# Later weight loads of the projections issued from ScalarE's queue instead of SyncE's

## The chip, the cores and the metric

The kernel runs on one core of a Trainium2 chip. What is measured is the device time of one execution in microseconds (us); before the change its median is 1826.89 us over three runs, which lie between 1826.79 and 1827.04. The engines are called as in the profile: PE (TensorE, matmuls) and PEld (its weight loads), DVE (VectorE), ACT (ScalarE), POOL (GpSimd) and SP (SyncE, which computes nothing and here issues DMA transfers). ACT can issue transfers too, from its own queue. Each engine works through its instructions in their order and waits where one of them needs another engine or a transfer.

## The reference

One layer of a decoder: a combined input projection feeds three token mixers, whose outputs go through one output projection, and a SwiGLU feed-forward network follows. There are 512 tokens of width 2048, all in float32.

```python
h = _rms_norm(x, norm1_g[l])
proj = h @ w_in[l]                                   # 2048 -> 3840 columns
aq, ak, av, bu, bg, cq, ck, cv = jnp.split(proj, splits, axis=-1)
out_a = _dilated_mixture(aq, ak, av)                 # 8 heads, three window/dilation patterns
out_b = _conformer_conv(bu, bg, ...)                 # GLU, 31-tap causal conv, LayerNorm, swish
out_c, _ = _band_attention(cq, ck, cv, ..., sinks)   # 16 query heads on 2 kv heads, window 128
x = x + concatenate([out_a, out_b, out_c]) @ w_out[l]
h2 = _rms_norm(x, norm2_g[l])
x = x + (silu(h2 @ w_gate[l]) * (h2 @ w_up[l])) @ w_down[l]
```

The queries and keys of a and c are normalised per head.

## The kernel before, in words

Activations lie with channels on the 128 partitions and the 512 tokens along them. Every float32 product is made of three matmuls: an operand is split into a high part (a cast to the matmul's own format) and a low part (what the cast left over), and `mm3` (lines 328 to 330) multiplies high by high, high by low and low by high.

**Stages.** Until about 50 us the first four column tiles of the input projection run together, k by k, as x arrives. Then `project` makes the other 26 column tiles one after the other (to about 375 us). Into these matmuls the attention of heads c and a, the convolution's taps and the normalisations are woven: a list of due times (`Ticks`) calls their pieces, one tick for every two k steps of a projection. Most pieces that move data across partitions go through DRAM and back (tiles named ..d and ..t, such as `c4ed` and `a1et`), by transfers that SP issues. The output projection follows (tiles named `o`, about 375 to 563 us) in two halves of sixteen tiles, each half over eight of the sixteen mixer rows; `residual` (line 1166) adds a finished bank into `xr`, the rows of x. The feed-forward network takes the rest, in seven products per block with sums and differences of weights made by POOL.

**Weights.** A weight unit is a tile of 128 x 1024 float32, 512 KB in one transfer (the first five are parts of such a tile). Units 0 to 10 are the first four column tiles, units 11 to 62 the other 26, two each, and units 63 to 94 the output projection, one per tile and half. Units of the feed-forward network have tuples as keys. Each unit has a raw buffer assigned beforehand (`RAW_PLAIN`, `RAW_FEWER`; from unit 51 to 90 five buffers in turn, since the attention of heads a uses two of the others). A unit's way is this: `pump` (line 237) takes its buffer if that is free and issues the load on line 249; `split_up_to` (line 269) has ACT cast the high part, `wh` (line 295), and keeps the subtraction of the low part in a list; `lows_now` (line 259) has DVE subtract, `wl` (named by line 269 in the profile); and PE multiplies. The split runs two units ahead of use (`SPLIT_AHEAD`), into three buffers each for `wh` and `wl`, so that a cast also waits until PE has finished a unit three back.

**Order around a load.** During the projections (`cooling`) `lows_now` is called in the middle of a unit; it frees buffers that were split one or two units before, pumps, and then subtracts. In the output projection nothing cools. `next_unit` runs in this order there:

```python
lows_now()                    # DVE subtracts the unit split last; its buffer is free; pump loads into it
split_up_to(u + SPLIT_AHEAD)  # ACT casts the next unit
```

Every load names an engine whose queue issues it, `eng` of `pump`. It is SP in all but the first call, where ACT issues four loads. A load waits in its queue until its buffer's last reader, the subtraction, is done. Transfers signal their end on eight semaphores that are handed out in turn, and a transfer also waits for the one before it on its semaphore.

The names that come up below: `c4e`, the exponentials of a pair of c heads on ACT (line 884); `c7by`, their scales spread over partitions by a transfer (line 842); `c4pl`, low parts of weights that POOL masks (line 935) for PE's `c4o` (line 1031); `a1et`, weights of an a pair coming back from DRAM (line 983), and `a1ph`, ACT's cast of them (line 993); `mh_c` and `ml_c`, the split mixer rows (lines 1085 and 1086).

Of the kernel before, what the change touches and what calls it, by code (L numbers as in the profile page):

```python
# [60 lines left out]
SPLIT_BUFS = 3  # L61
X_AHEAD = 8
SPLIT_AHEAD = 2
WARM = 8


# [55 lines left out]
def kernel(ctx: ExitStack, tc: tile.TileContext, xT, wi, wo, wgu, wd, cst_in, outT):  # L122
    nc = tc.nc
# [22 lines left out]
    def bank(name, cols=T, pool="banks"):  # L146
        return psum[pool].tile([P, cols], F32, name=name, tag="b")
# [11 lines left out]
    def take(buf, key, n=1024):  # L159
        assert buf not in held  # L160
        held[buf] = key
        raws[key] = (wp.tile([P, 1024], F32, name=f"w{key}", tag=f"raw{buf}", bufs=1), n)
        return raws[key][0]
# [25 lines left out]
    for n in range(2 * NBLOCKS):  # L189
# [6 lines left out]
        for i, c in enumerate("AB"):  # L196
            key = keys[c]
# [43 lines left out]
    def pump(limit, most=99, eng=nc.sync):  # L241
        while at["entry"] < len(entries) and len(raws) < limit and entries[at["entry"]][0] not in held and most:
            most -= 1
            buf, key, parts = entries[at["entry"]]
            size = [part.shape[-1] * (part.shape[1] if len(part.shape) == 3 else 1) for part in parts]
            t, o = take(buf, key, sum(size)), 0
            for part, n in zip(parts, size):
                to = t[:, o:o + n]
                eng.dma_start(to.rearrange("p (n f) -> p n f", n=part.shape[1]) if len(part.shape) == 3 else to, part)
                o += n  # L250
            at["entry"] += 1

# [10 lines left out]
    def lows_now():  # L263
        if lows and cooling:
            release()
            pump(RAW_EARLY if at["use"] <= 20 else RAW_BUFS)
        while lows:
            fn, *args = lows.pop(0)
            fn(*args)  # L269
        if late_lows and not cooling:  # L270
            pump(RAW_EARLY if at["use"] <= 20 else RAW_BUFS)

    def split_up_to(i):
        while at["split"] <= min(i, len(works) - 1):
            key, last, eng = works[at["split"]]
            of = [b for b, k in held.items() if k == key]
            t, n = drop(key) if last else raws[key]
            if cooling:
                held.update((b, None) for b in of)
                cool.extend(of)  # L280
            u = at["split"]
            hi = wp.tile([P, 1024], F32R, name=f"wh{u}", tag="hi", bufs=SPLIT_BUFS)
            lo = wp.tile([P, 1024], F32R, name=f"wl{u}", tag="lo", bufs=SPLIT_BUFS)
            if eng == "moves":

                near = psum["high"].tile([P, 1024], F32R, name=f"wn{u}", tag="h")
                src = t[:, :n].rearrange("p (n f c) -> p f n c", n=4, c=P)
                by = lambda x: x[:, :n].rearrange("p (f n c) -> p f n c", n=4, c=P)
                nc.scalar.copy(by(near), src)
                nc.scalar.copy(by(hi), src)  # L290
                nc.vector.tensor_sub(by(lo), src, by(near).bitcast(F32))
            elif eng or "high" not in psum:
                eng = eng or nc.vector

                (nc.vector.tensor_copy if u == 0 else nc.scalar.copy)(hi[:, :n], t[:, :n])  # L295
                lows.append((eng.tensor_sub, lo[:, :n], t[:, :n], hi[:, :n].bitcast(F32)))
                if not late_lows:
                    lows_now()
            else:
                near = psum["high"].tile([P, 1024], F32R, name=f"wn{u}", tag="h")  # L300
                nc.scalar.copy(near[:, :n], t[:, :n])
                nc.scalar.copy(hi[:, :n], t[:, :n])
                lows.append((nc.vector.tensor_sub, lo[:, :n], t[:, :n], near[:, :n].bitcast(F32)))
                if not late_lows:
                    lows_now()
            splits[u] = (hi, lo)
            at["split"] += 1
# [5 lines left out]
    def next_unit():  # L313
        sums_now()
        u = at["use"]
        at["use"] += 1
        moves = works[u][2] == "moves"
        ahead = moves and u < turned_to
        if ahead:
            pump(RAW_BUFS, 2)  # L320
        lows_now()
        split_up_to(u + SPLIT_AHEAD)
        if not lows and not ahead:
            pump(RAW_EARLY if u < 20 else RAW_BUFS, 2 if moves else 99)
        return splits.pop(u)
# [26 lines left out]
    b = bank("idle")  # L352
    for i in range(WARM):
        nc.tensor.matmul(b, idle, idle[:, None, :].to_broadcast([P, NT, P]), start=True, stop=True)
# [890 lines left out]

    split_up_to(at["use"] + SPLIT_AHEAD - 1)
    ticks.tick()
    split_up_to(at["use"] + SPLIT_AHEAD)
    b = m_hi = m_lo = r1b = bias_a = bias_c = over = upper = None
# [30 lines left out]
    def run(queue):  # L1280

        for fn, *args in queue.pop(0) if queue else ():
            fn(*args)
# [231 lines left out]
    for n in range(NBLOCKS):  # L1515
        blk = Up(n)
        for blk.first in (0, 4):
            for i, q in enumerate(ORDER):
                for c, _ in enumerate(blk.product(q)):
# [5 lines left out]
                    if 1 <= n <= 8 and at_unit in (9, 23):  # L1525
                        key = SUMS[2 * n - 2 + at_unit // 16]
# [32 lines left out]
    class Down:  # L1559
# [9 lines left out]
        def product(self, k, q):  # L1569
# [5 lines left out]
            for c in range(2):  # L1575
                sums_now()
                if self.end and k == 5:
                    split_up_to(at["use"] + SPLIT_AHEAD)
                run(evacs)
# [62 lines left out]
        def sum(self, i, k, a):  # L1642
            return self.g, i, k, a
# [149 lines left out]
```

## Time and profile before

| | |
|---|---|
| median of the runs | 1826.89 us |
| profiled execution: its own time | 1827.03 us |
| its span, first to last instruction | 1825.3 us |
| mean granted clock of TensorE | 0.999 |
| DMA queue q1 (SP): packets, MB | 408576, 352.12 |
| DMA queue q10 (ACT): packets, MB | 576, 0.79 |
| moved bytes over the span | 194 GB/s |

The profile is one execution. A row of a timeline gives start and duration in us, engine, line, operation and the tiles written and read; a remark in brackets gives the idle time before and what ended it. A row of waits has who waited, for whom, the sum in us, how often, and the longest. SPq and ACTq are the queues' own instructions: the issue of a transfer (DMA_DIRECT2D) and waiting for a semaphore (EVENT_SEMAPHORE), which are not counted as busy time.

### The profile page before, as it was taken

The numbers are of one execution on the slowest core, as the hardware profiler recorded it, in microseconds if no ns is written. First come the engines' busy times: TensorE is split into PE (matmuls) and PEld (weight loads), VectorE is DVE, ScalarE is ACT, GpSimd is POOL, SyncE is SP. The second block draws the span as 40 slices with busy tenths as digits, with TensorE's granted clock in tenths as the row PEclk, the third lists the DMA queues.
The fourth block names the chain that finished last, engine by engine and source line by source line (L and its number), as shares of the span: only waits on it lengthen the run. The fifth ranks groups of instructions, "written<-read, shape, count | busy, mean of one in ns | idle before, by whom it ended". The sixth has DMA issues, their size and how long they took to land.

```text
span 1825.3 us, 26570 instructions
## 1 busy us (share of the span) xinstructions
PE 1818.3 (100%) x8191; PEld 1509.9 (83%) x8191; DVE 1434.5 (79%) x1996; ACT 1327.6 (73%) x1848; POOL 1022.1 (56%) x793
## 2 busy tenths in 40 slices
PE   9999999999999999999999999999999999999998
PEld 7888888888888888888888888888888888888887
DVE  6779999987689777777777777777777777777777
ACT  6345656664468778888888888888887778877775
POOL 0116555120014577786887868878775568775652
PEclk9999999999999999999999999999999999999999
DMA  7355456666343557787777877778687579877645
GB/s 279 96 161 157 152 172 182 195 211 214 130 145 113 130 142 206 191 222 192 194 205 191 220 192 197 204 190 223 176 278 261 195 230 293 259 256 255 231 127 105
DMA packets 409295, 354.61 MB, mean 194 GB/s; under 512 B 177088, under 2 KB 331840, under 8 KB 409152
## 3 DMA queue, kind: packets, MB, share of 16 engines
q1 hardware_dynamic: 408576, 352.12, 65.7%
q8 instruction: 65, 1.06, 0.2%
q10 hardware_dynamic: 576, 0.79, 0.1%
q14 instruction: 78, 0.64, 0.1%
HBM read 270.00 MB, written 74.41 MB: 189 GB/s over the span
## 4 chain that ended last, share of the span: by engine, by line
PE 99%; DVE 1%; DMA 0%; issue 0%; ACT 0%; SPq 0%; DVEq 0%; ACTq 0%
PE out L1374 15%; PE out L1375 15%; PE out L1372 15%; PE out L1637 7%; PE out L1639 7%; PE out L1638 7%; PE o L328 3%; PE o L330 3%; PE o L329 3%; PE cq L328 2%; PE cq L329 2%; PE cq L330 2%; PE ak L328 1%; PE aq L328 1%; PE av L328 1%; PE ak L330 1%
## 5 line engine op out<-in xcount | busy, mean ns | idle before, releaser
L1372 PE MATMUL out<-wh,h 128*128 128x512 f32 x1232 | 479.2, 389 | 0.0
L1374 PE MATMUL out<-wl,h 128*128 128x512 f32 x1232 | 479.2, 389 | 0.0
L1375 PE MATMUL out<-wh,h 128*128 128x512 f32 x1232 | 479.2, 389 | 0.0
L1372 PEld LDWEIGHTS out<-wh,h 128*128 128x128 f32 x1232 | 231.2, 188 | 48.1
L1374 PEld LDWEIGHTS out<-wl,h 128*128 128x128 f32 x1232 | 231.2, 188 | 48.1
L1375 PEld LDWEIGHTS out<-wh,h 128*128 128x128 f32 x1232 | 231.2, 188 | 47.9
L1637 PE MATMUL out<-wh,a 128*128 128x512 f32 x620 | 240.4, 388 | 0.0
L1638 PE MATMUL out<-wl,a 128*128 128x512 f32 x620 | 240.3, 388 | 0.0
L1639 PE MATMUL out<-wh,a 128*128 128x512 f32 x620 | 240.3, 388 | 0.0
L295 ACT CAST wh<-w 128x1024 fp32r<-128x1024 f32 (+2 forms) x94 | 97.0, 1032 | 115.8 <-PE o L329 48.9
L1647 DVE TENSOR_TENSOR y<-y,out 128x512 f32<-128x512 f32 x192 | 128.6, 684 | 47.6 <-PE out L1639 46.1
L269 DVE TENSOR_TENSOR wl<-w,wh 128x1024 fp32r<-128x1024 f32 (+2 forms) x95 | 114.1, 1203 | 30.0 <-ACT wh L295 28.9
L1639 PEld LDWEIGHTS out<-wh,a 128*128 128x128 f32 x620 | 116.4, 188 | 24.0
L1638 PEld LDWEIGHTS out<-wl,a 128*128 128x128 f32 x620 | 116.4, 188 | 23.8
L1637 PEld LDWEIGHTS out<-wh,a 128*128 128x128 f32 x620 | 116.4, 188 | 23.8
L590 DVE SCALAR_TENSOR_TENSOR y<-bu,cst,y 128x511 f32<-128x511 f32 (+14 forms) x120 | 89.8, 748 | 0.5
L328 PE MATMUL o<-mh_c,wh 128*128 128x512 f32 x128 | 50.3, 393 | 0.0
L328 PE MATMUL cq<-hh,wh 128*128 128x512 f32 x128 | 50.0, 391 | 0.0
L329 PE MATMUL cq<-hl,wh 128*128 128x512 f32 x128 | 49.9, 390 | 0.0
L329 PE MATMUL o<-ml_c,wh 128*128 128x512 f32 x128 | 49.9, 390 | 0.0
L330 PE MATMUL o<-mh_c,wl 128*128 128x512 f32 x128 | 49.9, 390 | 0.0
L330 PE MATMUL cq<-hh,wl 128*128 128x512 f32 x128 | 49.8, 389 | 0.0
(2359 smaller groups left out, 4736.4 us busy)
## 6 DMA issues: line engine op xcount, KB each, us to landing
od<-a SPq DMA_DIRECT2D x154, 256.0 KB
a<-od SPq DMA_DIRECT2D x154, 256.0 KB
w<-in_wi SPq DMA_DIRECT2D x58, 512.0 KB
w<-in_wo SPq DMA_DIRECT2D x32, 512.0 KB
x<-in_xT SPq DMA_DIRECT2D x16, 256.0 KB
xr<-in_xT SPq DMA_DIRECT2D x16, 256.0 KB
x2d<-xr SPq DMA_DIRECT2D x16, 256.0 KB
z<-x2d SPq DMA_DIRECT2D x64, 64.0 KB
```

The costliest lines, as they stand in the source:

```text
L269: fn(*args)
L295: (nc.vector.tensor_copy if u == 0 else nc.scalar.copy)(hi[:, :n], t[:, :n])
L328: nc.tensor.matmul(out, wh, xh, start=start, stop=False)
L329: nc.tensor.matmul(out, wh, xl, start=False, stop=False)
L330: nc.tensor.matmul(out, wl, xh, start=False, stop=stop)
L1372: nc.tensor.matmul(b, x[:, high], wh[:, s], start=c == f == 0 and q in (7, 1, 5, 2), stop=False, skip_group_check=True)
L1374: nc.tensor.matmul(b, x[:, high], wl[:, s], start=False, stop=False, skip_group_check=True)
L1375: nc.tensor.matmul(b, x[:, low], wh[:, s], start=False, stop=c == f == 1, skip_group_check=True)
L1637: nc.tensor.matmul(b[:, lo:hi], x[:, high], wh[:, s], start=start, stop=False, skip_group_check=True)
L1638: nc.tensor.matmul(b[:, lo:hi], x[:, high], wl[:, s], start=False, stop=False, skip_group_check=True)
L1639: nc.tensor.matmul(b[:, lo:hi], x[:, low], wh[:, s], start=False, stop=last, skip_group_check=True)
L1647: getattr(eng, op)(t, t, src)
```

## The change

Loads whose key is a plain number of 46 or more are issued by ACT, whatever engine the call of `pump` names. Unit 46 is the second half of the first `aq` tile; from there on it is 17 units of the input projection and all 32 of the output projection. The loads keep their place in the order of the program, their buffers and their sizes. Loads of the feed-forward network have tuples as keys and stay on SP.

```diff
+ACT_LOADS = 46
...
                 to = t[:, o:o + n]
-                eng.dma_start(to.rearrange("p (n f) -> p n f", n=part.shape[1]) if len(part.shape) == 3 else to, part)
+                by = nc.scalar if isinstance(key, int) and key >= ACT_LOADS else eng
+                by.dma_start(to.rearrange("p (n f) -> p n f", n=part.shape[1]) if len(part.shape) == 3 else to, part)
                 o += n
```

## The prediction

> **What bounds the kernel now.** I read the first part of the page, then what TensorE (PE) waited for, then the stretches of time in which the moved loads are issued.
>
> ```profile
> PE 1818.3 (100%) x8191; PEld 1509.9 (83%) x8191; DVE 1434.5 (79%) x1996; ACT 1327.6 (73%) x1848; POOL 1022.1 (56%) x793
> PE idle L354 <- DVE nhalf L360: 1.1, 1, 1.1
> PE sides L1602 <- DVE y L1616: 1.1, 2, 0.6
> 205.00:300.00 95.00, 95.00 (x475) 80.69 (x474) 88.82 (x175) 51.52 (x123) 52.64 (x88) 1.00 0.55 165
> 357.00:375.00 18.00, 18.00 (x88) 15.29 (x87) 15.74 (x25) 8.85 (x16) 6.06 (x3) 1.00 0.81 219
> 375.00:415.00 40.00, 40.00 (x190) 33.51 (x189) 35.05 (x83) 27.82 (x65) 3.36 (x4) 1.00 0.66 205
> 415.00:455.00 40.00, 40.00 (x189) 33.40 (x188) 28.03 (x46) 17.22 (x29) 0.00 (x0) 1.00 0.66 212
> ```
>
> The columns of the last four rows are the stretch in us, its length, and the busy time of PE, PEld, DVE, ACT and POOL, then the granted clock, the DMA share and GB/s. PE is busy for 1818.3 of 1825.3 us. Its only two waits stand at the very start and the very end of the program, and in every stretch shown it is busy from end to end at full clock. So PE is the bound, and nothing that happens between 205 and 510 us can take time out of it; the 7.0 us of idle time lie elsewhere. The change can only cost, and it costs where it makes something late that PE needs. The second thing to see is DVE: 88.82 of 95.00, 15.74 of 18.00, 35.05 of 40.00. It has little idle time in which to catch up, while ACT has plenty.
>
> **What moves.** The next rows are the instructions of the load line and what held SP's queue there; the three numbers are shortest, median and longest in ns, then first and last start.
>
> ```profile
> L249 SPq EVENT_SEMAPHORE  x399: 17/28/9942, 9.0 to 1777.3; - x200
> L249 SPq DMA_DIRECT2D w<-in_wo x32: 328/360/1634, 337.5 to 510.8; - x32
> L249 ACTq DMA_DIRECT2D w<-in_wi x4: 417/452/453, 0.8 to 2.2; - x4
> SPq L249 <- DVE wl L269: 74.5, 24, 10.0
> SPq L760 <- DMA w<-in_wo: 2.6, 2, 1.4
> ```
>
> Units 46 to 94 are the last 17 loads of the input projection and all 32 of the output projection: 49 issues, and each is one DMA. They leave SP, whose time is not on PE's path, and come to ACT. The issue itself has a row on ACT, the four at the start: 0.45 us. That makes 49 x 0.45 = 22 us of ACT's queue. Alone I cost it at nothing: ACT is busy 27.82 us of 40 in the densest stretch, and 20 issues there would still fit. Without that cover the 22 us would be the price.
>
> The waits are another matter. A load may not overwrite its buffer before the unit that lies there has been split, so it waits for DVE's subtraction (wl, line 269). On SP that wait lasted up to 9.9 us and only other transfers stood behind it. On ACT all of ACT's work stands behind it: the next weight cast, the exponentials and the evacuations, and DVE waits for these in turn. In the output projection the order is written in the code: lows_now issues the subtraction, then pump issues the load into that buffer, then split_up_to issues the next cast. So from now on ACT's next cast starts after DVE's subtraction has ended, where so far it ran ahead of it. A second wait comes along: each transfer waits until an earlier one that used the same completion semaphore has landed (the fifth row: SP's copies of k, which touch no weights, waited for a weight load). The program hands out eight of them in turn, so a load on ACT also waits for a transfer eight places earlier, mostly one of SP's.
>
> **The cost, by places.** First the stretch 382 to 410 us, where five moved loads of the output projection fall. Rows are start, duration, engine, line and operation; the first fence has DVE's subtractions, the second the ACT cast that comes behind the load.
>
> ```profile
> 385.12 1.22 DVE L269 TENSOR_TENSOR wl<-w,wh 128x1024 fp32r<-128x1024 f32 x1
> 389.66 1.22 DVE L269 TENSOR_TENSOR wl<-w,wh 128x1024 fp32r<-128x1024 f32 x1
> 394.36 1.22 DVE L269 TENSOR_TENSOR wl<-w,wh 128x1024 fp32r<-128x1024 f32 x1
> 400.11 1.22 DVE L269 TENSOR_TENSOR wl<-w,wh 128x1024 fp32r<-128x1024 f32 x1
> 405.40 1.22 DVE L269 TENSOR_TENSOR wl<-w,wh 128x1024 fp32r<-128x1024 f32 x1
> 407.17 0.68 DVE L1166 TENSOR_TENSOR xr<-xr,o 128x512 f32<-128x512 f32 x1
> ```
>
> ```profile
> 383.08 1.05 ACT L295 CAST wh<-w 128x1024 fp32r<-128x1024 f32 x1
> 387.90 1.05 ACT L295 CAST wh<-w 128x1024 fp32r<-128x1024 f32 x1 [0.60 <-PE o L329]
> 393.79 1.06 ACT L295 CAST wh<-w 128x1024 fp32r<-128x1024 f32 x1 [0.52 <-PE o L329]
> 400.31 1.06 ACT L295 CAST wh<-w 128x1024 fp32r<-128x1024 f32 x1 [0.60 <-PE o L329]
> 406.20 1.06 ACT L295 CAST wh<-w 128x1024 fp32r<-128x1024 f32 x1 [1.72 <-PE o L329]
> 414.00 0.40 PE L328 MATMUL o<-mh_c,wh 128*128 128x512 f32 x1
> ```
>
> Take the first pair: the subtraction ends at 386.34, the load needs 0.45, so the cast starts at 386.79 at the earliest and not at 383.08: 3.7 us late. The other four give 3.4, 2.2, 1.5 and 0.9: together 11.7 us. Before them comes the load at the end of the attention, whose eighth transfer before it is the third of four a1et:
>
> ```profile
> 359.18 0.62 ACT L1085 CAST mh_c<-mix_c 128x512 fp32r<-128x512 f32 x1 [2.12 <-PE a1o L1030]
> 364.21 1.14 ACT L993 CAST a1ph<-a1et 128x512 fp32r<-128x512 f32 x2
> 358.16 2.02 SPq L983 DMA_DIRECT2D a1et<-a1ed  x4
> ```
>
> It landed after its issue (360.2 at the latest) and before its reader started (364.2). In the middle, 362.2, ACT would take up mh_c at 362.65, 3.5 us late; the ends are 1.5 and 5.5, and 0 if the turn of the semaphores comes out otherwise. I take 3.5.
>
> How much of these 15.2 us stays? DVE is what passes them on, since ACT's casts and logits feed its queue in order. Its idle time from 357 to 415 is 18.00 - 15.74 + 40.00 - 35.05 = 7.2 us. All of it used would leave 8.0, none 15.2. Idle time that lies ahead of a late piece cannot take it up, so I count half, 3.6, and have DVE 11.6 us late at 408. There it adds a finished bank into the residual (xr, ending at 407.85), and PE's next product into that bank starts at 414.00. The slack is 6.15 us, and PE loses 11.6 - 6.15 = **5.5 us**. With all the idle time used it is 1.9, with none 9.1.
>
> Then the layer norm's stretch:
>
> ```profile
> 445.23 1.05 ACT L295 CAST wh<-w 128x1024 fp32r<-128x1024 f32 x1 [3.96 <-issue]
> 446.45 1.22 DVE L269 TENSOR_TENSOR wl<-w,wh 128x1024 fp32r<-128x1024 f32 x1
> 449.78 0.68 DVE L1166 TENSOR_TENSOR xr<-xr,o 128x512 f32<-128x512 f32 x1
> 451.91 0.40 PE L328 MATMUL o<-mh_c,wh 128*128 128x512 f32 x1
> ```
>
> DVE's idle 40.00 - 28.03 = 12.0 us from 415 to 455 brings it back to the delayed PE. But here the load has to wait until 447.67, the cast comes at 448.12 instead of 445.23, 2.9 us late, and the squares behind it feed DVE's sum just ahead of xr. The slack is 451.91 - 450.46 = 1.45: PE loses **1.5 us** (0 if DVE's own order hides the squares, 2.9 without slack).
>
> In the projections the loads lie in ACT's idle time (51.52 busy of 95.00), but one stands in a loop:
>
> ```profile
> 259.27 0.46 ACT L884 ACTIVATE c4e<-c4s,c4d,cq4r 128x128 f32<-128x128 f32 x1 [3.24 <-DVE c4d L878]
> 256.50 2.14 SPq L842 DMA_DIRECT2D c7by<-c7sums  x2
> 263.35 0.69 DVE L846 TENSOR_TENSOR mix_c<-mix_c,c7by 128x512 f32<-128x512 f32 x1
> 283.31 0.71 POOL L935 TENSOR_SCALAR_AFFINE_SELECT c4pl<-c4lp 128x128 fp32r<-128x128 f32 x1
> 286.44 0.28 PE L1031 MATMUL c4o<-c4pl,cv 128*128 128x256 f32 x1
> ```
>
> Its eighth transfer before it is the second c7by, landed between 258.6 and 263.35; at the middle, 261.0, the exponentials c4e start at 261.45, 2.2 us late, and the round trip through memory and POOL behind them too. The slack before PE reads c4pl is 286.44 - 284.02 = 2.4, so PE loses **nothing** at the middle; at the late end, 263.35, the exponentials are 4.5 us late and PE loses 4.5 - 2.4 = 2.1.
>
> SP gives up 49 x 0.36 = 18 us of issuing and the waits behind it; its transfers come a little earlier, which PE does not notice as it waits for none. The sum is 5.5 + 1.5 = 7.0 us. The profiled execution took 1827.03 us, 0.14 above the median of 1826.89 (its span is 1825.3): 1834.0 against it, **1833.9** against the median.
>
> **The rivals.** *No change that counts.* ACT's and DVE's idle time swallows the late pieces one by one, and only the place at 451.91, which needs no accumulation, costs its 1.5 us: 1828.4. For it speaks that ACT is idle for 12.2 of 40 us in the densest stretch and that the weights are split two units ahead; against it DVE at 88% with its order fixed. The Trainium skill, "DMA: Bandwidth & Descriptors", section "Issuing engines are not separate DMA queues", says that starting DMAs from several engines saves only the initiating sequencer's time, which is usually small: by that rule the sum is 0 and the time 1826.9. Chance 0.26 for times up to 0.2% above.
>
> *The two queues lock.* SP's transfers get their turn behind loads that ACT has not issued yet, so the attention's round trips stand behind ACT, which stands behind DVE. For it speaks the fifth row of the load line, where k's copies already wait for weights; against it that these waits sum to 2.6 us. It would decide once ACT is further behind than a transfer's turn. With no idle time used (9.1), the long end of the landing (2.0 more), 1.5 and 2.1 it gives 14.7 us: 1841.6. Chance 0.14.
>
> *Faster.* SP's transfers no longer stand 74.5 us behind subtractions, and something late for PE comes earlier. PE would have to be waiting for it, and it is not in any stretch shown; even the whole 7.0 us of idle would give 1819.9. Chance 0.02.
>
> That the change does not do what it says is hardly possible: keys below 46 and the tuple keys of the later weights stay with SP, and the rest is one call.
>
> **How the numbers follow.** My forecast has 0.58. A measurement can tell about 0.2%, 3.7 us, from no change: 1830.5 is the line. Forecast and lock lie above it, 0.72; the swallowed case below, 0.26; faster 0.02. The range reaches from the single place, 1828.4, to the lock, 1841.6.
>
> **What would show it.** In the profile after, queue q10 carries 49 x 0.52 = 25.7 MB more; ACT's waits list its load line behind DVE wl and DMAs, at least the 20.3 us of the late pieces above (15.2 + 2.9 + 2.2); DVE waits more for ACT; PE gets waits near 414 and 452 on DVE, of 7 us together, and perhaps one near 286 on POOL. If PE still waits for nothing there, the late pieces were swallowed and the forecast is wrong. If PE waits for a transfer of SP, it was the lock.

## The result, and the profile after

The changed kernel takes 1841.67 us, the median of four runs between 1840.37 and 1842.75, against 1826.84 us for the kernel before on the same chip: a ratio of 1.0081, with a 95% interval from 1.0064 to 1.0099. That is 14.8 us more. The forecast was 7.0 us more, and the measured time lies 0.07 us above the upper end of the range. Lines of the program stand two further down than before (the load is on line 251, the cast on 297, the subtraction on 271, xr on 1168).

From the page after, engines and queues:

```profile
span 1839.6 us, 26566 instructions
PE 1821.9 (99%) x8191; PEld 1511.1 (82%) x8191; DVE 1435.2 (78%) x1996; ACT 1327.0 (72%) x1848; POOL 1022.3 (56%) x793
q10 hardware_dynamic: 7632, 26.48, 4.3%
```

What PE waited for (sum in us, times, longest):

```profile
PE o L330 <- DVE xr L1168: 9.4, 4, 3.6
PE a2s L865 <- DMA aq<-aq2l: 1.4, 1, 1.4
```

And the stretches, in the columns of the prediction:

```profile
300.00:357.00 57.00, 57.00 (x275) 47.90 (x274) 51.14 (x108) 37.23 (x79) 16.83 (x21) 1.00 0.67 190
357.00:375.00 18.00, 16.63 (x80) 13.80 (x79) 14.33 (x24) 8.38 (x14) 1.42 (x2) 1.00 0.88 235
375.00:415.00 40.00, 36.61 (x170) 30.03 (x169) 29.92 (x67) 22.30 (x52) 7.40 (x6) 1.00 0.68 207
415.00:455.00 40.00, 40.00 (x187) 33.44 (x187) 30.14 (x59) 18.57 (x35) 0.00 (x0) 1.00 0.65 208
455.00:485.00 30.00, 24.03 (x101) 19.28 (x100) 18.28 (x26) 13.93 (x20) 1.01 (x1) 0.91 0.23 79
```

Queue q10 has gained 25.7 MB, so the change does what it says. PE now has five waits more: 1.37, 2.15, 1.24, 2.39 and 3.59 us by its timeline, 10.7 us together (the last four are the 9.4 of the first row). They end at 370, 391, 398, 459 and 482 us; in the profile before, the same matmuls ran at 369.6, 387.9, 393.8, 451.9 and 469.2, and by these times the places are called below. PE is still busy from end to end between 300 and 357 and between 415 and 455. So nothing is lost in the projections up to 357, and nothing at 414.

The waits don't make up the whole loss. PE's busy time has grown by 3.6 us with the same 8191 matmuls, and in the last stretch the granted clock is 0.91. The place of 451.9 shows both things. First ACT there, then DVE:

```profile
453.68 0.33 ACTq L251 DMA_DIRECT2D w<-in_wo  x1
454.12 1.05 ACT L297 CAST wh<-w 128x1024 fp32r<-128x1024 f32 x1 [5.80 <-DVE wl L271]
455.60 1.66 ACT L427 ACTIVATE lq<-y 128x512 f32<-128x512 f32 x3
```

```profile
452.10 1.20 DVE L271 TENSOR_TENSOR wl<-w,wh 128x1024 fp32r<-128x1024 f32 x1
456.25 2.29 DVE L428 TENSOR_TENSOR lnv<-lnv,lq 128x512 f32<-128x512 f32 x3 [2.94 <-ACT lq L427]
458.45 0.68 DVE L1168 TENSOR_TENSOR xr<-xr,o 128x512 f32<-128x512 f32 x1
```

The issue of the load stands in ACT's queue until after the subtraction has ended (452.10 + 1.20 = 453.30). ACT has been idle for 5.80 us when its cast starts at 454.12. The squares lq come behind the cast, DVE's sum lnv waits 2.94 us for them, and xr comes behind the sum. Before, DVE went from the subtraction to the sum without a pause. PE at that place:

```profile
459.18 0.79 PE L330 MATMUL o<-mh_c,wh 128*128 128x512 f32 x1 [2.39 <-DVE xr L1168]
...
460.20 0.63 PE L332 MATMUL o<-mh_c,wl 128*128 128x512 f32 x1
460.63 0.63 PE L330 MATMUL o<-mh_c,wh 128*128 128x512 f32 x1
```

PE waits 2.39 us, and then its matmuls start 0.43 us apart (460.20 and 460.63 in the rows) instead of 0.23, until about 462.3. The same is seen behind the wait of 3.59 us that ends at 481.81: from 482.81 to 486.19 they start 0.43 apart. Some eight matmuls, 0.2 us late each, make about 1.6 us a place (an estimate from these rows), 3.2 us of the 3.6 by which PE's busy time has grown. That growth and the waits (10.7) are the 14.3 us by which the two profiled spans differ.

### The profile page after: what moved, and what is told of

Read it like the earlier page. It is cut to its first block, busy times and chain, and to the rows that moved or that the text cites. A ratio compares the mean times of both kernels' runs of the same rounds, so it can differ in the third digit from the quotient of the medians.

```text
span 1839.6 us, 26566 instructions
## 1 busy us (share of the span) xinstructions
PE 1821.9 (99%) x8191; PEld 1511.1 (82%) x8191; DVE 1435.2 (78%) x1996; ACT 1327.0 (72%) x1848; POOL 1022.3 (56%) x793
## 4 chain that ended last, share of the span: by engine, by line
PE 73%; DVE 1%; issue 0%; DMA 0%; ACT 0%; DVEq 0%
PE out L1374 15%; PE out L1377 15%; PE out L1376 15%; PE out L1640 7%; PE out L1639 7%; PE out L1641 7%; PE o L330 2%; PE o L331 2%; PE o L332 2%; DVE y L1649 0%; DVE wl L293 0%; DMA out_T<-z 0%; DVE z L1548 0%; DVE y L1618 0%; PE sides L1604 0%
```

## The experiments

Three causes came up. **A**: a load waits in ACT's queue for DVE's subtraction, and the work of ACT behind it comes late. **C**: ACT's loads among the attention's round trips make SP's transfers late. **K**: PE runs slowly for a while behind some of its waits. In the expectations A always means the first. B, C and D, in the first eight texts, are other ways in which ACT's loads could cost, above all by SP's transfers (their turns, sharing, getting ahead); from e9 on C takes all of these together. A code cut leaves out lines where it has three dots; where one cut stands for several runs, the text says what differs. All comparisons are with the kernel before, at 1826.4 to 1827.0 us on the same chip.

### A: the wait for the subtraction

**e1.** All loads stay on SP; in the output stage ACT copies one column of the low part at the place of the load, so that it waits for the same subtraction. It does so only where the load's buffer is the one whose subtraction was issued last: 23 times, first at 386.68 us, so not yet at the first loads of the stage.

```diff
+            if isinstance(key, int) and key >= ACT_LOADS and last_low and last_low[0] == buf:
+                nc.scalar.copy(seen, last_low[1][:, :1].bitcast(F32))
...
-                by = nc.scalar if isinstance(key, int) and key >= ACT_LOADS else eng
+                by = eng
```

> All loads are back on SP. In the output projection ACT copies one column of the unit's low part into a scratch tile where the changed kernel has its load, so that it waits for DVE's subtraction there and issues nothing (an added copy; the result is not touched). Theory A, ACT's queue stands behind DVE's subtraction and hands the delay on: PE waits for xr near 388, 394, 452 and 469 as in the changed kernel, the time is 8 to 13 us above the kernel before, about 1838. Rival B, loads and SP's transfers wait for each other by the turn of the completion semaphores: nothing is left of it, 1827 to 1829. Rival C, the issue time of 0.45 us and a second stream of transfers: 1827 to 1829 as well.

It took 1832.86 us (ratio 1.0039, 1.0024 to 1.0053): 6.4 us of the 14.8, with no load on ACT. PE's waits of it, and the longest:

```profile
PE o L335 <- DVE xr L1173: 4.3, 3, 3.0
```

```profile
474.22 0.47 PE L335 MATMUL o<-mh_c,wh 128*128 128x512 f32 x1 [3.02 <-DVE xr L1173]
```

The wait alone makes xr late, at the places of 393.8, 451.9 and 469.2; this is less than the expectation gave to A, and less than half of the loss, so A in this form is not everything. And here no slow matmul follows a wait of 3.02 us. (PE also waits 0.6 us for a cast at 263.9; the runs don't show why.)

**e2.** The loads are on ACT, but in the output stage each is put one unit later into its queue, when its subtraction is done (but for unit 68, see e10).

```diff
         if late_lows and not cooling:
-            pump(RAW_EARLY if at["use"] <= 20 else RAW_BUFS)
+            held_back[0] = loads_due(RAW_BUFS)
+            if not held_back[0]:
+                pump(RAW_EARLY if at["use"] <= 20 else RAW_BUFS)
...
+        if held_back[0]:
+            n, held_back[0] = held_back[0], 0
+            pump(RAW_BUFS, n)
```

> All 49 loads stay on ACT. In the output projection each load stands one unit later in ACT's queue, at the end of the unit during which DVE subtracts, so that the subtraction is done when ACT comes to it. Theory A: the waits for xr go, the early wait for a query's copies (1.4 us near 370) stays, 1828 to 1831. Rival B: the turn of the semaphores is nearly the same, so is the time, 1838 to 1843. Rival C: the issues and the second stream are all there, 1838 to 1843.

It took 1830.53 us (1.0026, 1.0015 to 1.0036). PE's waits of the output stage:

```profile
PE o L345 <- DVE xr L1183: 1.9, 1, 1.9
PE a2s L880 <- DMA aq<-aq2l: 1.1, 1, 1.1
```

The waits at 398, 459 and 482 are gone, and with them some 11 of the 14.8 us. What stays are the places of 369.6 and 387.9.

### Which loads the rest belongs to

**e3 and e4** split the loads by stage: only the output projection's (63 and up, the cut shown), and only those of the projections (46 to 62).

```diff
-ACT_LOADS = 46
+ACT_LOADS = 63
```

> Only the 32 loads of the output projection go to ACT, from unit 63 on. Theory A: the four waits for xr and the slow matmuls behind two of them stay, 1838 to 1841. Rival B with the projection's loads at its root: the delay begins with the query copies near 370, so without the 17 earlier loads most of it goes, 1830 or less. Rival C goes by the number of issues: 32 of 49 of 14.8 us, 1836.5.

> Only the 17 loads of the input projection from unit 46 on go to ACT. Theory A: these loads find their subtraction done long before, so only the wait for a query's copies near 370 is left, 1827 to 1829. Rival B: PE is late from 370 on and DVE with it, 1832 to 1838. Rival C: 17 of 49 of 14.8 us, 1832.

e3 took 1841.38 us (1.0081, 1.0066 to 1.0096), e4 1826.39 us (1.0001, 0.9991 to 1.0010), and in e4 PE waits for nothing new. The 17 loads of the projections cost nothing, though one does what the locked queues were said to do. In the kernel after, SP's queue has this wait in a copy of k:

```profile
SPq L661 <- DMA w<-in_wi: 2.8, 1, 2.8
```

A transfer of SP that touches no weights waited 2.8 us for ACT's load of unit 62. With that load on ACT (e4) PE lost nothing; it had slack enough. In e3 the wait at 369.6 is the longest of its places:

```profile
PE a2s L865 <- DMA aq<-aq2l: 4.7, 1, 4.7
```

After it PE doesn't wait at 387.9 and 393.8. In the kernel after, the waits of the three places sum to as much (1.37, 2.15 and 1.24): lateness that PE has waited out at one place is not paid again at the next.

**e5 and e6** put unit 66 alone back on SP, which ACT issues just ahead of SP's transfers for `aq` (e6: in the order of e2).

```diff
-                by = nc.scalar if isinstance(key, int) and key >= ACT_LOADS else eng
+                by = nc.scalar if isinstance(key, int) and key >= ACT_LOADS and key != 66 else eng
```

> As the changed kernel, but the load of unit 66 alone goes back to SP, 48 loads on ACT. Theory D, overtaking: from ACT this load starts at 360.3 us, 4 us earlier than on SP, and shares the DMA engines with the copies of k and q that it used to follow on SP's queue, so these land later. Then the wait for the query's copies near 370 (1.4 us) goes, the one for xr at 388 shrinks, and 452 and 469 stay: 1836 to 1839. Theory B, turns of the semaphores in general: one load of 49 changes little, 1840 to 1842.

> 48 loads on ACT, those of the output projection one unit later in its queue (as in the run at the unit's end) and the load of unit 66 on SP. If waiting for the subtraction (A) and overtaking by unit 66 (D) are the whole cost, nothing is left: 1826 to 1828, with no wait of PE between 205 and 570. If issues and a second queue cost by themselves (C) or the turns do (B), 1829 to 1831 as without the last step.

e5 took 1841.40 us (1.0079, 1.0063 to 1.0094) and e6 1829.86 us (1.0019, 1.0009 to 1.0028). In e5's profile the wait at 369.6 is gone, in e6's 0.2 us of it stays, but the wait at 387.9 remains in both (2.3 us in e6). So unit 66 alone is not the cause of the rest, and both expectations that were built on it fall. The wait at 369.6 is also missing in e9's profile, where nothing was changed at that place, so one profile without it proves little.

**e7 and e8** add to the kernel before one spare transfer of ACT at that place, 512 KB or 4 KB.

```diff
+            if key == 66:
+                nc.scalar.dma_start(spare, wo[0][:, :1024])
...
```

> The kernel before, with one added transfer of 512 KB that nothing reads, from weights in DRAM to scratch DRAM, issued by ACT at the place of unit 66; no load is moved and ACT waits for no subtraction. D: it fills the DMA engines while the copies of k and q are under way; PE waits for the query's copies near 370, 1 to 5 us, 1828 to 1832. A: nothing, 1826 to 1827.5.

> The same added transfer, cut to 4 KB: the same place, the same taking of a turn, nearly no bytes. D: nothing, 1826 to 1827.5. B: what the large one costs, it costs too.

They took 1826.43 us (0.9999, 0.9990 to 1.0009) and 1826.40 us (1.0000, 0.9991 to 1.0010). One more transfer of either size at this place (357 to 358 us in the traces) costs nothing.

### C: the loads among the round trips

**e10 to e13** are the kernel of e2 with some loads back on SP: 63 to 67 (e10), 62, 64 and 66 (e11), 63 to 68 (e12, the cut shown), and 68 alone (e13).

```diff
-                by = nc.scalar if isinstance(key, int) and key >= ACT_LOADS else eng
+                by = nc.scalar if isinstance(key, int) and key >= ACT_LOADS and not 63 <= key <= 68 else eng
```

> Loads from 46 on by ACT, those of the output stage one unit later in its queue so that their subtraction is done, but units 63 to 67 by SP. With them on ACT this was 1830.5. C (what is left there comes from the few loads that ACT issues among SP's round trips of the last attention pairs, some us ahead of the place that they had in SP's queue): 1826 to 1828, and PE waits for nothing in the output stage. Rival, what is left comes from ACT's later loads, or from the subtraction after all: 1829 to 1831, with PE's wait near 388 for DVE's xr still there.

> As the one before it, but only units 62, 64 and 66 go back to SP; 63, 65 and 67 stay on ACT. By the trace of the changed kernel, unit 62 is the one behind whose landing a transfer of SP (k's copy, 334.5) waits for its turn, and 64 and 66 are those that are issued ahead of SP's a0by, a1et and aq2d and share the transfers' time with them. C in this narrow form: 1826 to 1828, no PE wait near 370 and 388. C in a wide form (any of the five loads among the round trips costs): 1828 to 1830, with part of the wait near 388 left.

> As the kernel with units 63 to 67 on SP and the later loads one unit later in ACT's queue (1830.2), but unit 68 on SP too. In that kernel's trace ACT issued unit 68 at 376.19, right after the subtraction that ended at 376.21, and took up the logits a2s at 376.63 instead of 374.33. C with A at this one place (the round trips made late by 62 to 67, and the load of unit 68 that waits for a subtraction): 1826 to 1828, no PE wait in the output stage. Rival, 46 loads on ACT's queue cost in themselves, or the place one unit later does: 1829 to 1831, and PE's wait near 388 stays.

> All loads from 46 on by ACT, those of the output stage one unit later, only unit 68 on SP. C (the five loads 63 to 67 among SP's round trips make the normaliser aq2r late, for which ACT then waits): PE's wait near 388 stays and the time is 1829 to 1831, as with unit 68 on ACT (1830.5). A alone (the wait for the subtraction in front of load 68 is what is left): 1826 to 1828 and no PE wait near 388.

e12 took 1827.07 us (1.0002, 0.9993 to 1.0010) and e13 1832.62 us (1.0031, 1.0019 to 1.0043). e12 is clean, and e13 has both waits:

```profile
PE o L345 <- DVE xr L1183: 2.5, 1, 2.5
PE a2s L880 <- DMA aq<-aq2l: 1.2, 1, 1.2
```

The two differ in loads 63 to 67 alone, so these are the cause of the two waits in e13. How they do it is seen in SP's queue. The copy that a2s needs was issued by SP at these times, before, in e4 and after:

```profile
363.20 0.47 SPq L702 DMA_DIRECT2D aq<-aq2l  x1
```

```profile
364.53 0.47 SPq L704 DMA_DIRECT2D aq<-aq2l  x1
```

```profile
367.93 0.47 SPq L704 DMA_DIRECT2D aq<-aq2l  x1
```

Some 24 us earlier SP is already late in both, by 3.0 us in e4 (a0by issued at 341.81, before at 338.78) and by 4.0 in the kernel after. In e4 it makes up for most of that. In the kernel after it does not. There ACT issues unit 64 at the moment at which SP issues a0by, while in e4 and before SP issues it behind them. ACT's row, SP's rows and one of SP's waits, all of the kernel after:

```profile
342.81 0.35 ACTq L251 DMA_DIRECT2D w<-in_wo  x1
```

```profile
342.83 1.09 SPq L844 DMA_DIRECT2D a0by<-a0sums  x2
...
346.31 4.98 SPq L780 DMA_DIRECT2D av2s<-av2d  x4
```

```profile
SPq L780 <- DMA a0by<-a0sums: 3.5, 2, 2.4
```

The issue of the four av2s, 1.73 us before, took 4.98, because they waited 3.5 us for a0by, which they don't read: a wait for their turn behind transfers that landed late. ACT's logits a2s wait for the normaliser that comes back by one of SP's round trips. Before they started at 374.33; after, and in e12:

```profile
378.30 0.82 ACT L943 ACTIVATE a2s<-a2s,aq2r 128x128 f32<-128x128 f32 x2 [5.45 <-POOL aq2r L676]
```

```profile
374.55 0.82 ACT L958 ACTIVATE a2s<-a2s,aq2r 128x128 f32<-128x128 f32 x2 [2.80 <-POOL aq2r L691]
```

The 3.97 us reach xr through DVE, and PE at 387.9.

e10 took 1830.15 us (1.0019, 1.0009 to 1.0028), as its rival said and not as C did: here one of the later loads costs, by its subtraction after all. ACT issued unit 68 at 376.19 behind a subtraction (in e2's order too this one load still meets a fresh one), and a2s started at 376.63: A at one more place. Unit 68 on SP as well is e12 (1.0002 against 1.0019). Units 68 and 63 to 67 don't add up in the order of e2: e2 has both and takes no more than e13. Both make the same xr late, and each alone is enough for it. e11 took 1828.81 us (1.0014, 1.0005 to 1.0022), by the wide form of its expectation; PE waits 0.5 us at 387.9. Which of the five loads does how much was not told apart; of the ways, e14's trace shows one, the turn.

### Do they add, and K

**e14 and e15** take the two parts by themselves in the changed kernel's own order: only 63 to 67 on ACT (the cut shown), and all but 63 to 67.

```diff
-                by = nc.scalar if isinstance(key, int) and key >= ACT_LOADS else eng
+                by = nc.scalar if isinstance(key, int) and 63 <= key <= 67 else eng
```

> The kernel before with only units 63 to 67 issued by ACT, at their old places in the program. C (these five loads make SP's round trips late, and PE waits near 370 and 388): 1829 to 1833, the waits there as in the changed kernel, none near 452 and 469. Rival, the five cost only together with the later loads: 1826 to 1828, no wait.

> The changed kernel with units 63 to 67 back on SP, the later loads of the output stage on ACT at their places in the program. If the two parts add (C 3 to 6 us, A with the slow matmuls the rest): 1836 to 1839, no wait near 370, waits near 452 and 469 as in the changed kernel. If C's delay is only swallowed by the waits of A behind it: 1840 to 1842, as the changed kernel.

e14 took 1830.51 us (1.0023, 1.0014 to 1.0031), 4.1 us more than before, and e15 1839.31 us (1.0068, 1.0054 to 1.0081), 12.9 us more. Together 16.9 against 14.8. The interval of the latter reaches from 11.7 to 18.1 us, so it does not tell whether the parts add; e15's 1839.31 lies between what the two theories gave, just above the adding one. In e14 PE waits at 369.6 (1.0 us) and 387.9 (1.3 us, put down to the cast wh). Two of SP's waits there:

```profile
SPq L733 <- DMA w<-in_wo: 3.8, 1, 3.8
SPq L727 <- DMA w<-in_wo: 1.9, 1, 1.9
```

These are copies of k (ak2wide, ak3e), which read no weights. They go out when ACT's units 63 and 64 have landed, which used the same completion semaphores before them. So in e14 part of C is a wait for a turn, 5.7 us of SP's queue in the two places; in the kernel after, the rows above show such waits behind unit 62 and among SP's own transfers.

In e15 PE waits at 387.9 (2.31 us), 451.9 (1.95) and 469.2 (3.59), and slow matmuls follow the first two. The first place is not the subtraction's doing alone. ACT's rows there:

```profile
376.99 0.33 ACTq L251 DMA_DIRECT2D w<-in_wo  x1
377.43 0.82 ACT L943 ACTIVATE a2s<-a2s,aq2r 128x128 f32<-128x128 f32 x2 [6.25 <-DMA ak3l<-ak3lo]
```

The load is unit 68. Its subtraction had ended at 374.83 and POOL's normaliser at 374.59, but it went out at 376.99, when a copy of k (ak3l), SP's transfer before it on its semaphore, had landed; a2s stood behind it, at 377.43 instead of 374.33. That is the second wait of the prediction. In e1 ACT doesn't wait there (a2s starts at 374.63), nor PE at 387.9. So A in its narrow sense, the subtraction, is shown by e1 (6.4 us); the 12.9 us of e15 also hold this turn and two stretches of slow matmuls.

**e9** is the changed kernel with eight spare matmuls ahead of the output tiles that wait at 459 and 482. Their result is used nowhere.

```diff
+            if half == 0 and i in (12, 15):
+                spare = bank(f"spare{i}")
+                for _ in range(8):
+                    nc.tensor.matmul(spare, m_hi[ROWS[0]][:, :P], m_hi[ROWS[0]], start=True, stop=True)
...
```

> The changed kernel with eight spare matmuls (a high part times itself, into a spare bank; their result is used nowhere) before the first matmul of the output tiles that wait at 459 and 482 us. K (behind a wait PE's granted clock falls for some us, and that costs 3.2 us at these two places beside the 6 us of the waits): the spare matmuls fill most of each wait, the granted clock stays at full speed there, no run of matmuls at 0.63 us follows, and the time falls by about 3 us, to 1837.5 to 1839.5. Rival, the slowness comes with the data or with what the other engines do just then: the spare matmuls change nothing of it or add up to 2 us, 1841 to 1844, and the granted clock dips as before.

It took 1838.08 us (1.0061, 1.0049 to 1.0074), 3.6 us below the changed kernel's 1841.67, though it does more work. PE at the two places:

```profile
455.00 2.00 PE L1234 MATMUL spare<-mh_c 128*128 128x512 f32 x8
457.47 0.50 PE L330 MATMUL o<-mh_c,wh 128*128 128x512 f32 x1 [0.47 <-DVE xr L1168]
```

```profile
474.87 1.97 PE L1234 MATMUL spare<-mh_c 128*128 128x512 f32 x8
478.65 0.47 PE L330 MATMUL o<-mh_c,wh 128*128 128x512 f32 x1 [1.81 <-DVE xr L1168]
```

At the first place the wait is filled to 0.47 us and no slow matmul follows; some 1.6 us are saved. At the second 1.81 us of waiting are left and the slow matmuls come all the same, from 480.10 to 483.48. Half of K's expectation holds, then: with most of the wait gone the slowness goes, so it does not come with the data. One profile would not show this, since equal waits can end either way (last section). But in the traces of all runs none of the fifteen waits of PE under 1.8 us between 200 and 570 us is followed by slow matmuls, and ten of the eighteen longer ones are. Most of the rest of the 3.6 us lies at 369.6, where PE did not wait in e9's profile; why not is open, since nothing was changed there.

## Why the prediction was wrong in size

**What bounds the kernel, and the direction.** PE was the bound, and the change could only cost. This held in every run: no kernel is faster than the one before by more than the interval.

**The issues at nothing.** Right. e12 has 43 loads on ACT (17 and 26) and takes 1827.07 us. There the rule of the Trainium skill, "DMA: Bandwidth & Descriptors", section "Issuing engines are not separate DMA queues", holds: issuing from several engines saves only the sequencer's time. For the changed kernel, where the rule's 1826.9 stands against 1841.67, it leaves out what the issuing engine waits for.

**The wait for the subtraction.** The mechanism was right (e1, e2). At least 20.3 us of waits behind the load line were forecast, for wl and DMAs together. The list of ACT's waits gives 15.7 us to wl, but more of them are its doing:

```profile
ACT wh L297 <- issue: 20.1, 7, 3.6
ACT wh L297 <- DVE wl L271: 15.7, 5, 5.8
```

Between 375 and 485 us 15 casts stand idle behind a load, 45 us in all (three of them are listed under matmuls and a transfer), and 14 of these loads go out within 0.1 us of the end of a subtraction, the last within 0.4. Not all of the 45 us is lateness: before, these casts waited too, mostly for PE.

**The wait for a turn.** Right as a mechanism, wrong in its places. At 360 us 3.5 us were taken; mh_c came 1.6 us late there (360.78 against 359.18), behind a copy of k and not a1et. The exponentials c4e, for which 2.2 us were taken, came 0.35 us late (259.62 against 259.27). Unit 68 in e15, 2.2 us past its subtraction, was not listed.

**The stretch 382 to 410: this step failed.** I summed up lateness until 408 and set it against the slack of 6.15 us at 414.00. PE did not wait there at all. A chain of late pieces reaches PE first where the slack is smallest, and there are tighter places in the trace of before:

```profile
386.25 0.68 DVE L1166 TENSOR_TENSOR xr<-xr,o 128x512 f32<-128x512 f32 x1
391.91 0.69 DVE L1166 TENSOR_TENSOR xr<-xr,o 128x512 f32<-128x512 f32 x1
467.94 0.68 DVE L1166 TENSOR_TENSOR xr<-xr,o 128x512 f32<-128x512 f32 x1
```

```profile
387.93 0.39 PE L328 MATMUL o<-mh_c,wh 128*128 128x512 f32 x1
393.82 0.39 PE L328 MATMUL o<-mh_c,wh 128*128 128x512 f32 x1
469.23 0.39 PE L328 MATMUL o<-mh_c,wh 128*128 128x512 f32 x1
```

The slacks are 1.00, 1.22 and 0.61 us. PE waited at all three. That the first stretch, with the place of 369.6, lost 4.8 us of waiting (1.37, 2.15 and 1.24) where 5.5 were forecast is near by chance: a good part is the round trips of e14.

**The layer norm's stretch.** The place and the chain (cast, squares, sum, xr) were right, and 1.5 us became 2.39 of waiting and 1.6 of slow matmuls.

**The place of 469.23 was left out.** The same pattern, with mh_b in place of the squares, stands there with a slack of 0.61 us. It cost 3.59 us and 1.6 of slow matmuls: 5.2 of the 7.8 us by which the sum was short. For slow matmuls the sum had no term at all; they cost about 3.2 us at the two places.

**"SP's transfers come a little earlier, which PE does not notice."** Wrong. The copy of 363.20 came 4.7 us later, and loads 63 to 67 alone, which make SP late, cost 4.1 us (e14).

**The projections at nothing.** Right (e4).

**The rivals.** The locked queues were priced at 1841.6, almost what was measured, but not by this way. Its mechanism exists: between 200 and 500 us in the kernel after, SP's queue waits four times for a turn behind a load of ACT (2.6 us at 295, 2.8 at 334, 0.3 at 425, 5.0 at 445), and in e14 5.7 us. But the part of the loss that comes by SP's late round trips, turns and all, is 4.1 us, not 14.7, so the near hit in time is luck. The swallowed case falls: lateness reaches PE at five places.

## What to carry to other kernels

Before a DMA issue is moved to a compute engine, look for what it waits for: the issue costs that engine next to nothing, but its wait stops everything queued behind it. To price such a wait, list every hand-over to the engine that bounds the kernel with its slack, and let the lateness reach the tightest first; the widest tells nothing. And a second queue changes when transfers start and behind which other one each waits for its turn, so look at the round trips that had the first queue for themselves.

## What was not expected of the hardware

A wait of PE can cost more than its length: behind it matmuls may start 0.43 us apart instead of 0.23, for up to 3.4 us, and in e3 and e5 once for 5.1 us. It doesn't go by the length of the wait. The wait of 2.39 us at 459 in the kernel after, and the 1.81 us in e9, were followed by it; the 3.02 us in e1 were not. Two waits of 3.59 us before the same matmul ended differently, with eight slow matmuls in the kernel after and none in e15. What differs is how the wait lies on a fixed grid. In the traces the granted clock changes only at steps of 3.41 us: in the kernel after it is 0.50 from 458.92 to 462.34 and from 482.82 to 486.23, and the 20.48 us between are six such steps. Three steps around the wait of 3.59 us, in the kernel after and then in e15 (columns as before):

```profile
475.99:479.40 3.41, 2.23 (x10) 1.50 (x8) 2.38 (x4) 0.98 (x2) 0.00 (x0) 1.00 0.02 2
479.40:482.82 3.42, 1.01 (x5) 0.87 (x6) 2.45 (x4) 0.94 (x2) 0.00 (x0) 1.00 0.41 151
482.82:486.23 3.41, 3.41 (x10) 2.64 (x9) 1.80 (x2) 1.05 (x1) 0.00 (x0) 0.50 0.47 159
```

```profile
475.82:479.23 3.41, 1.70 (x8) 1.08 (x6) 1.86 (x3) 1.15 (x2) 0.00 (x0) 1.00 0.13 31
479.23:482.64 3.41, 1.52 (x7) 1.30 (x8) 2.96 (x4) 0.50 (x2) 0.00 (x0) 1.00 0.31 123
482.64:486.05 3.41, 3.41 (x17) 2.80 (x16) 1.29 (x2) 0.97 (x1) 0.00 (x0) 1.00 0.57 172
```

In the first, 2.4 us of the wait fall into one step, and the next runs at half the clock; in the second the wait is shared out, 1.7 and 1.9 us, and nothing follows. The traces of all runs agree between 340 and 500 us: from full clock, each of the nine steps with 1.95 us or more of PE's waits was followed by half the clock, none with 1.80 or less was, and of three with 1.81 to 1.89 one was (e9).

The Trainium skill, "TensorE: Matmul & The Clock Gate", section "Part 1: The HAM clock gate (the "warmup" mystery)", says that the clock falls to half after an idle window of about 3.4 us, comes back after as long a busy one, and that the window runs freely. Its half rate, its 3.4 us and a free window agree with the granted clock and the grid here; that a whole idle window is needed does not, since PE was busy for 1.01 us of the 3.42 before the fall.
